# Weight sums of a Strassen quad moved into accumulating DMAs, and the LayerNorm residual moved ahead, in a two-layer decoder trunk on one core

## The chip, the cores and the metric

The kernel runs on one core of one Trainium2 chip. The time is the device time of one execution in microseconds (us): 2227.26 us is the median of three runs of the kernel before, which lie between 2225.66 and 2228.39 us.

## The reference, cut to what matters

Input is x, 256 tokens by 2048. Two layers follow each other; each is a token mixer and then a gated ConvFFN, and after each of the four sub-layers stands `x <- LayerNorm(ALPHA * x + sublayer(x))`. Layer 0 mixes with a gated linear recurrence (HGRN2), layer 1 with a causal spatial gating (gMLP). The change lies in the ConvFFN, which both layers have:

```python
h = x @ w_up                        # 2048 -> 2 * 5632
a, b = split(h, 2)
a = conv_w[0]*a[t-2] + conv_w[1]*a[t-1] + conv_w[2]*a[t] + conv_b
y = (silu(a) * b) @ w_down          # 5632 -> 2048
```

All of it is float32.

## The kernel before, in words

**Number form.** TensorE gets every float32 matrix as two float32r parts, `hi` (the rounded value) and `lo` (what is left), and a product is three matmuls: hi by hi, hi by lo, lo by hi. A weight chunk is 512 by 512 (1 MB). It is loaded into a buffer `raw` by a DMA of SyncE's queue (`begin_fetch`, L96), ScalarE casts it to `whi` in two halves (L120), VectorE subtracts to get `wlo` in two halves (L121). `raw`, `whi` and `wlo` have three buffers each, and `ahead(3)` (L128) issues loads and conversions up to three chunks ahead of the one that TensorE takes. So the conversion of a chunk can begin when TensorE has done with the chunk three places before it.

**The ConvFFN** (`ffn`, L1063) works through eleven F-chunks f of 512 hidden columns, in groups of 4, 3 and 4. For each F-chunk there are two blocks of four weight chunks ("ups"): the gate products for `a` (first `block_b`, L1112) and the products for `b` (second `block_b`, L1116). A block ends in an evacuation by ScalarE and VectorE: `ev_a` (gather, convolution, silu) and `ev_b` (gather, gate, split into `Y`). After a group come the "down" chunks of `w_down`, each 24 matmuls.

**The Strassen quads.** For column chunks 0 and 1 of `w_down` two F-chunks f, f+1 are taken together: the 2x2 blocks B11, B12 (first F-chunk), B21, B22 (second) of the weights against two halves of the tokens, in seven products of 12 matmuls each where eight would be plain (`seven`, L233; `product`, L210). The sums of activations are made by `sums` (L187) into a tile `S`. The sums of weights are made by `make` (L156), in place in two buffers `b11`, `b12` of a pool `qp`, which has one buffer of each. The products are numbered `which`; their order is 0, 1, 2, 3, 4, 6, 5:

- 0: load b11 = B11 and b12 = B12 by SyncE's queue (L154); convert b11; then b11 += b12 on VectorE (two halves, L165)
- 1: convert b11 (B11 + B12)
- 2: load b2 = B22 into a `raw` buffer, convert it; then b11 += b2 and b12 += b2 on VectorE
- 3: convert b11. 4: convert b12 (B12 + B22)
- 6: load b2 = B21; b11 += b2; convert b11. 5: convert b2

**What sets the order.** `ffn_order` (L1023) writes the order of the chunks by hand: ups and downs are counted from 0, and `QUADS` (L34) says behind which count each of the seven products of a quad stands. There are four quads in each layer, so eight in all. The instructions of each engine are laid out once, at build time, mostly in the order of the program, where something whose inputs are planned to be ready may pass something that is not; on the chip each engine runs its list strictly in that order.

**The residual and the memory of `qp`.** `norm` loads the LayerNorm's g and b as eight broadcast tiles into a pool on the right side of the memory. `residual(c)` (L551) applies them to column chunk c of z, four VectorE instructions each (L556, L557), placed behind the last conversion that was issued (`issue_after`). `residual(3)` closes the pool. `qp` opens in the same memory, so the loads of b11 and b12 of a layer's first quad wait for the residual's last instruction. Before, the residual of column chunks 0 and 1 stands behind the second block of F-chunk 0, and that of 2 and 3, with the opening of `qp`, behind the second block of F-chunk 1.

Of the kernel before, what the change touches and what calls it, by code (L numbers as in the profile page):

```python
# [12 lines left out]
ALU = mybir.AluOpType  # L13
# [6 lines left out]
DFF = 5632  # L20
# [5 lines left out]
NB = 512  # L26
CK = 4
# [4 lines left out]
SUMS = ((0, 1), (0, 3), (1, 2), (2, 1))  # L32
SEVEN = (0, 1, 2, 3, 4, 6, 5)
QUADS = (  # L34
# [4 lines left out]
)  # L39
# [12 lines left out]
class Trunk:  # L52
# [96 lines left out]
    def want_seven(self, w, k0, c0, which):  # L149
        self.plan.append((w, k0, c0, None, which))  # L150

    def load_chunk(self, raw, w, k0, c0):
        src = w[k0 * P : (k0 + CK) * P, c0 : c0 + NB].rearrange("(k p) n -> p k n", p=P)
        self.nc.sync.dma_start(raw, src)  # L154

    def make(self):  # L156

        w, k0, c0, _, which = self.plan[self.issued]
        self.issued += 1
        nc = self.nc  # L160

        def add(out, x, y):
            for i in range(0, CK, 2):
                r = slice(i, i + 2)
                nc.vector.tensor_tensor(out[:, r], x[:, r], y[:, r], ALU.add)  # L165

        if which == 0:
            self.b11 = self.qp.tile([P, CK, NB], F32, tag="b11", name="b11")
            self.b12 = self.qp.tile([P, CK, NB], F32, tag="b12", name="b12")
            self.qp.tile([P, PAD2], mybir.dt.uint8, tag="pad2", name="pad2")  # L170
            self.load_chunk(self.b11, w, k0, c0)
            self.load_chunk(self.b12, w, k0, c0 + NB)
        elif which in (2, 6):
            self.b2 = self.wp.tile([P, CK, NB], F32, tag="raw", name="raw")
            self.load_chunk(self.b2, w, k0 + CK, c0 + NB * (which == 2))
        if which == 6:
            add(self.b11, self.b11, self.b2)
        self.convert(
            self.b2 if which in (2, 5) else self.b12 if which == 4 else self.b11, False, False
        )  # L180
        if which == 0:
            add(self.b11, self.b11, self.b12)
        elif which == 2:
            add(self.b11, self.b11, self.b2)
            add(self.b12, self.b12, self.b2)

    def sums(self, act0, act1):  # L187

# [874 lines left out]
    def ffn(self, l, store=None):  # L1063
        nc, tc, a = self.nc, self.tc, self.a
        up, down = a["ffn_w_up"][l], a["ffn_w_down"][l]
        with ExitStack() as st:
            fp = st.enter_context(tc.tile_pool(name=f"fp{l}", bufs=2))
            m = 0
            quads = ExitStack()
            order = self.ffn_order(l)  # L1070
            slots = {}
            self.fresh = {(t, c) for t in range(2) for c in range(4)}

            def sevens():
                while order and order[0][0] == "seven":
                    _, f, which = order.pop(0)
                    self.seven(which, slots[f])

            def next_up(ci):
                assert order.pop(0)[::3] == ("up", ci)  # L1080
                sevens()

            for gi, n in enumerate(FFN_GROUPS):
                acts = []
                for i in range(n):
                    slot = slots[m + i] = FFN_SLOT[gi] + i
                    act = fp.tile([P, 4, S], F32, tag="act", name="act")
                    acts.append(act)

                    def ev_a(j, ps):  # L1090
                        f = 4 * (m + i) + j
                        x = fp.tile([P, S], F32, tag="a", name="a")
                        self.gather(fp, ps, x)
                        cv = act[:, j, :]
                        nc.vector.tensor_scalar(
                            cv, x, self.c(("cw", l, 2), f), self.c(("cb", l), f),
                            ALU.mult, ALU.add,
                        )
                        for d in (1, 2):
                            nc.vector.scalar_tensor_tensor(  # L1100
                                cv[:, d:], x[:, : S - d], self.c(("cw", l, 2 - d), f),
                                cv[:, d:], ALU.mult, ALU.add,
                            )
                        nc.scalar.activation(cv, cv, AF.Silu)

                    def ev_b(j, ps):
                        x = fp.tile([P, S], F32, tag="b", name="b")
                        self.gather(fp, ps, x)
                        nc.vector.tensor_tensor(act[:, j, :], x, act[:, j, :], ALU.mult)
                        self.split(self.Y, 4 * slot + j, act[:, j, :])  # L1110

                    self.block_b(self.X, up, 4, (m + i) * NB, ev_a, halves=m + i == 0,  # L1112
                                 between=next_up)
                    if m + i == 0:
                        self.xps.close()
                    self.block_b(self.X, up, 4, DFF + (m + i) * NB, ev_b, between=next_up)  # L1116
                    if m + i in (0, 1):
                        self.residual(2 * i)
                        self.residual(2 * i + 1)
                    if m + i == 1:  # L1120
                        self.qp = quads.enter_context(
                            tc.tile_pool(name=f"qp{l}", bufs=1, side="right")
                        )
                    if (gi, i) in SUMS:
                        self.sums(*acts[-2:])
                end = m + n == NF // CK
                if end:
                    quads.close()
                    st.close()
                    self.norm("ln2", l, store)  # L1130
                    for c in range(4):
                        fs = [x[1] for x in order if x[2] == c]
                        self.block_a(self.Y, slots[fs[0]] * CK, down, fs[0] * CK, len(fs), c * NB,
                                     self.add_z(c, last=True), staggered=c == 3)
                m += n
                while not end and order[0][0] == "down":
                    _, f, c, first, last = order.pop(0)
                    ch = self.chunk(down, f * CK, c * NB)
                    if first:
                        ps = [self.acc.tile([P, NB], F32, tag="acc", name="pa") for _ in range(2)]  # L1140
                    for t in range(2):
                        self.product(ps[t], self.half(slots[f], t), ch, first, last)
                    if last:
                        for t in range(2):
                            self.gain(t, c, ps[t])
                    sevens()
# [59 lines left out]
```

## Time and profile before

| | |
|---|---|
| median of three runs | 2227.26 us (2225.66 to 2228.39) |
| the profiled execution | 2227.53 us, of which the span from first to last instruction is 2225.8 us |
| TensorE matmul (PE) busy | 2198.7 us, 99% |
| TensorE weight load (PEld) busy | 1896.3 us, 85% |
| VectorE (DVE) busy | 1659.9 us, 75% |
| ScalarE (ACT) busy | 1171.8 us, 53% |
| GpSimd (POOL) busy | 46.8 us, 2% |
| granted TensorE clock, mean | 0.997 |
| DMA | 430.14 MB, 193 GB/s |

Lines of a profile name engine, source line, operation and `out<-in`. In a row of the timeline stand start, length, engine, line, operation, tiles, count, and in brackets the idle time before it with what ended it. In a row of groups stands behind the bar the busy time in us, the mean of one in ns, and the idle time before. In a row of windows stands for each engine busy time with its count, then granted clock (PEclk), DMA share and GB/s. SPq is SyncE's queue, which issues DMAs; L numbers are lines of the kernel.

### The profile page before, as it was taken

The page shows a single profiled execution, that of the slowest core. Times are in us where ns is not written, and L with a number is a line of the kernel's source. Part 1 is how long each engine was busy: PE and PEld are TensorE (multiplying, and loading weights), DVE is VectorE, ACT ScalarE, POOL GpSimd, SP SyncE. Part 2 cuts the span into 40 slices and gives each one's busy share as a digit, 9 for nine tenths or more (in the row PEclk, how much of TensorE's full clock was granted, in tenths as well). Part 3 has the DMA queues.
Part 4 walks back from the last instruction along what each step waited for, and adds up shares of the span by engine and source line. Part 5 has one row for each costly group of instructions (what it writes and reads, how often), then busy time and mean ns, then how long its engine had stood idle before and what let it go on. Part 6 is the DMA issues. An engine that isn't in the chain of part 4 may idle for free.

```text
span 2225.8 us, 31866 instructions
## 1 busy us (share of the span) xinstructions
PE 2198.7 (99%) x12705; PEld 1896.3 (85%) x12705; DVE 1659.9 (75%) x2533; ACT 1171.8 (53%) x1783; POOL 46.8 (2%) x102
## 2 busy tenths in 40 slices
PE   9999999999999999999999999999999999999998
PEld 8888888889788888888888888888788888888886
DVE  6877677668888676877876676567788676877875
ACT  5656575546445454555555545455455454545452
POOL 3000000000000000000000000000000000000000
PEclk9999999999999999999999999999999999999999
DMA  7454645645555665555565665655555656555573
GB/s 269 152 189 143 199 152 170 214 166 188 190 208 189 208 227 190 172 207 189 189 227 187 210 214 192 230 179 172 199 197 190 215 202 207 184 191 174 191 244 114
DMA packets 214597, 430.14 MB, mean 193 GB/s; under 512 B 7577, under 2 KB 9393, under 8 KB 214449
## 3 DMA queue, kind: packets, MB, share of 16 engines
q1 hardware_dynamic: 210080, 415.26, 55.0%
q0 software_dynamic: 4368, 12.85, 1.9%
q8 instruction: 99, 1.62, 0.3%
q14 instruction: 50, 0.40, 0.1%
HBM read 425.98 MB, written 2.10 MB: 192 GB/s over the span
## 4 chain that ended last, share of the span: by engine, by line
PE 92%; DVE 3%; ACT 2%; issue 2%; DMA 1%; POOL 0%; SPq 0%; DVEq 0%; POOLq 0%; ACTq 0%
PE pb L359 36%; PE pb L366 18%; PE pa L215 8%; PE px L215 7%; PE pa L282 6%; PE pa L283 6%; PE pa L281 6%; DVE wlo L121 1%; ACT whi L120 1%; PE pl L796 1%; PE pt L481 1%; DMA b<-in_ffn_w_down_dram 0%; PE pg L1005 0%; DVE z L557 0%; DMA bb<-in_sg_ln_b_dram 0%
## 5 line engine op out<-in xcount | busy, mean ns | idle before, releaser
L359 PE MATMUL pb<-X,whi 128*128 128x512 f32 (+1 forms) x3960 | 1306.1, 384 | 1.9 <-DVE X L495 1.9
L121 DVE TENSOR_TENSOR wlo<-raw,whi 128x1024 fp32r<-128x1024 f32 (+1 forms) x753 | 892.3, 1219 | 450.0 <-ACT whi L120 442.1
L120 ACT CAST whi<-raw 128x1024 fp32r<-128x1024 f32 (+1 forms) x753 | 760.2, 1048 | 697.6 <-PE pb L359 385.9
L366 PE MATMUL pb<-X,wlo 128*128 128x256 f32 x3840 | 1038.0, 278 | 0.0
L359 PEld LDWEIGHTS pb<-X,whi 128*128 128x128 f32 x3960 | 725.7, 188 | 144.0 <-DVE X L495 2.4
L366 PEld LDWEIGHTS pb<-X,wlo 128*128 128x128 f32 x3840 | 713.2, 188 | 7.2 <-DVE wlo L121 0.2
L282 PE MATMUL pa<-wlo,Y 128*128 128x512 f32 x416 | 162.3, 390 | 0.0
L281 PE MATMUL pa<-whi,Y 128*128 128x512 f32 x416 | 162.3, 390 | 0.0
L283 PE MATMUL pa<-whi,Y 128*128 128x512 f32 x416 | 162.0, 389 | 0.0
L215 PE MATMUL pa<-whi,Y 128*128 128x512 f32 x512 | 160.3, 389 | 0.0
L381 ACT COPY rest<-pb 128x256 f32<-128x256 f32 x240 | 87.3, 368 | 97.7 <-PE pb L359 94.7
L215 PEld LDWEIGHTS pa<-whi,Y 128*128 128x128 f32 x512 | 96.1, 188 | 19.7
L121 DVE TENSOR_TENSOR wlo<-b,whi 128x1024 fp32r<-128x1024 f32 x80 | 95.0, 1220 | 14.9 <-ACT whi L120 14.9
L120 ACT CAST whi<-b 128x1024 fp32r<-128x1024 f32 x80 | 80.9, 1050 | 43.0 <-PE pb L359 13.9
L282 PE MATMUL pa<-wlo,X 128*128 128x512 f32 x256 | 99.9, 390 | 0.0
L281 PE MATMUL pa<-whi,X 128*128 128x512 f32 x256 | 99.8, 390 | 0.0
L215 PE MATMUL pa<-wlo,Y 128*128 128x512 f32 x256 | 99.7, 389 | 0.0
L283 PE MATMUL pa<-whi,X 128*128 128x512 f32 x256 | 99.7, 389 | 0.0
L281 PEld LDWEIGHTS pa<-whi,Y 128*128 128x128 f32 x416 | 78.1, 188 | 16.0
L282 PEld LDWEIGHTS pa<-wlo,Y 128*128 128x128 f32 x416 | 78.1, 188 | 16.0
L283 PEld LDWEIGHTS pa<-whi,Y 128*128 128x128 f32 x416 | 78.1, 188 | 15.9
L215 PE MATMUL px<-whi,S 128*128 128x512 f32 x256 | 84.2, 390 | 2.8 <-ACT whi L120 2.8
(191 smaller groups left out, 1816.3 us busy)
## 6 DMA issues: line engine op xcount, KB each, us to landing
raw<-in_ffn_w_up_dram SPq DMA_DIRECT2D x176, 1024.0 KB, 5.0
raw<-in_ffn_w_down_dram SPq DMA_DIRECT2D x72, 1024.0 KB, 4.9
raw<-in_hg_w_in_dram SPq DMA_DIRECT2D x61, 1024.0 KB, 5.0
raw<-in_sg_w_in_dram SPq DMA_DIRECT2D x32, 1024.0 KB, 5.4
raw<-in_hg_w_out_dram SPq DMA_DIRECT2D x16, 1024.0 KB, 4.9
b<-in_ffn_w_down_dram SPq DMA_DIRECT2D x16, 1024.0 KB, 4.9
raw<-in_sg_w_out_dram SPq DMA_DIRECT2D x16, 1024.0 KB, 4.9
g<-in_ln_g_dram POOLq DMA_DIRECT2D x16, 256.0 KB, 5.9
```

Of the source, the lines that this page charges most:

```text
L120: cast = nc.scalar.copy(hi[:, s, :], raw[:, s, :])
L121: self.last_lo = nc.vector.tensor_tensor(lo[:, s, :], raw[:, s, :], hi[:, s, :].bitcast(F32), ALU.subtract)
L215: self.nc.tensor.matmul(ps, x(kk, part), y[:, kk, :], start=start and (kk, part) == (0, 0) and y is hi, stop=stop and (kk, part) == (CK - ...
L281: nc.tensor.matmul(ps[t], xh, hi[:, kk, :], start=n[t] == 0, stop=False)
L282: nc.tensor.matmul(ps[t], xh, lo[:, kk, :], start=False, stop=False)
L283: nc.tensor.matmul(ps[t], xl, hi[:, kk, :], start=False, stop=last)
L359: return self.nc.tensor.matmul(ps[j][:, :, s], ch[0][:, k % CK, c], act[:, k, :, s], start=start and k == 0, stop=k == last, skip_group_ch ...
L366: return self.nc.tensor.matmul(ps[j][:, 1, :], ch[1][:, k % CK, c], act[:, k, 0, :], start=False, stop=False, skip_group_check=loose,)
L381: nc.scalar.copy(r, ps[:, 1, :])
L481: self.last_turn = nc.tensor.transpose(ps[:, j, :], self.z[:, t, k * P : (k + 1) * P], self.ident)
L796: nc.tensor.matmul(ps[n * j : n * j + n, th, :], K[:, own(th, n, j)], moving(th, j), start=True, stop=True, tile_position=(0, n * j),)
```

## The change

Three things are edited. First, two of the four weight sums of a quad become DMAs that add into their destination (`accum_op`), issued by GpSimd: b12 += B22 right behind the load of b12 in step 0, and b11 += B12 behind the conversion of b11 in step 0. The VectorE sums b11 += b12 (step 0) and b12 += b2 (step 2) go; b11 += b2 in steps 2 and 6 stays. Second, `residual(2)`, `residual(3)` and the opening of `qp` move from behind the second block of F-chunk 1 to behind its first block (the gate products). Third, in the first two quads of a layer most of the seven products stand one count later.

```diff
 QUADS = (
-    (0, (17, 19, 22, 24, 26, 28, 30)),
-    (2, (32, 34, 37, 40, 42, 45, 47)),
+    (0, (18, 20, 23, 25, 27, 29, 31)),
+    (2, (33, 35, 38, 40, 43, 45, 47)),
     (5, (65, 67, 70, 73, 76, 79, 82)),
     (7, (89, 91, 94, 96, 98, 100, 102)),
 )
...
-    def load_chunk(self, raw, w, k0, c0):
+    def load_chunk(self, raw, w, k0, c0, add=False):
         src = w[k0 * P : (k0 + CK) * P, c0 : c0 + NB].rearrange("(k p) n -> p k n", p=P)
-        self.nc.sync.dma_start(raw, src)
+        if add:
+            self.nc.gpsimd.dma_start(raw, src, accum_op=ALU.add)
+        else:
+            self.nc.sync.dma_start(raw, src)
...
             self.load_chunk(self.b11, w, k0, c0)
             self.load_chunk(self.b12, w, k0, c0 + NB)
+            self.load_chunk(self.b12, w, k0 + CK, c0 + NB, add=True)
...
         if which == 0:
-            add(self.b11, self.b11, self.b12)
+            self.load_chunk(self.b11, w, k0, c0 + NB, add=True)
         elif which == 2:
             add(self.b11, self.b11, self.b2)
-            add(self.b12, self.b12, self.b2)
...
-                    self.block_b(self.X, up, 4, DFF + (m + i) * NB, ev_b, between=next_up)
-                    if m + i in (0, 1):
-                        self.residual(2 * i)
-                        self.residual(2 * i + 1)
                     if m + i == 1:
+                        self.residual(2)
+                        self.residual(3)
                         self.qp = quads.enter_context(
                             tc.tile_pool(name=f"qp{l}", bufs=1, side="right")
                         )
+                    self.block_b(self.X, up, 4, DFF + (m + i) * NB, ev_b, between=next_up)
+                    if m + i == 0:
+                        self.residual(0)
+                        self.residual(1)
```

## The prediction

> **What bounds the kernel now.** I read the page first, its busy times.
>
> ```profile
> span 2225.8 us, 31866 instructions
> PE 2198.7 (99%) x12705; PEld 1896.3 (85%) x12705; DVE 1659.9 (75%) x2533; ACT 1171.8 (53%) x1783; POOL 46.8 (2%) x102
> ```
>
> TensorE is the bound: all its idle time is 2225.8 - 2198.7 = 27.1 us. The matmuls themselves are not touched by the change, so it can win only what TensorE waits for. The second view is the list of TensorE's own waits; its first line and its fourth carry most of what lies in the ConvFFN.
>
> ```profile
> PE px L215 <- ACT whi L120: 7.1, 4, 2.1
> ...
> PE px L215 <- DVE wlo L121: 1.5, 2, 0.8
> ```
>
> Both are waits of `px`, that is of Strassen products, 8.6 us in six stalls. The third view, the timeline of PE, shows where: in each layer at the first quad only, products 0 and 1. In layer 0:
>
> ```profile
> 602.85 0.39 PE L359 MATMUL pb<-X,whi 128*128 128x512 f32 x1
> 605.37 0.50 PE L215 MATMUL px<-whi,Y 128*128 128x512 f32 x1 [2.13 <-ACT whi L120]
> 606.62 0.50 PE L215 MATMUL px<-wlo,Y 128*128 128x512 f32 x1 [0.76 <-DVE wlo L121]
> ...
> 611.05 0.50 PE L215 MATMUL px<-whi,S 128*128 128x512 f32 x1 [1.62 <-ACT whi L120]
> 611.39 0.28 PE L366 MATMUL pb<-X,wlo 128*128 128x256 f32 x1
> ```
>
> In layer 1:
>
> ```profile
> 1598.36 0.39 PE L359 MATMUL pb<-X,whi 128*128 128x512 f32 x1
> 1600.88 0.50 PE L215 MATMUL px<-whi,Y 128*128 128x512 f32 x1 [2.14 <-ACT whi L120]
> ...
> 1607.83 0.28 PE L366 MATMUL pb<-X,wlo 128*128 128x256 f32 x1
> ```
>
> The price of these two places is the time between the last block matmul and the next one, less what the 13 products between them (12 of product 0, one of product 1) need at full pace. The pace is a row of the chain in an undisturbed stretch:
>
> ```profile
> 712.05 10.88 PE pa L215 x48
> ```
>
> 10.88 / 48 = 0.227 us for one matmul. Layer 0: from 602.85 + 0.227 to 611.39 are 8.31 us, 13 x 0.227 = 2.95 of it work: 5.36 us lost. Layer 1: from 1598.36 + 0.227 to 1607.83 are 9.24 us, less 2.95: 6.29 us lost. Together 11.65 us. That is more than 8.6 since matmuls after a wait also run slower; in layer 1 the windows show why:
>
> ```profile
> 1602.00:1604.00 2.00, 1.86 (x4) 1.49 (x5) 2.00 (x3) 2.00 (x3) 0.00 (x0) 0.50 0.00 0
> ```
>
> The granted clock falls to 0.50 there, and not in layer 0 after the same waits. The Trainium skill ("TensorE: Matmul & The Clock Gate", Part 1) says that the gate judges activity in a free-running window of about 3.4 us, so that it depends on the phase whether such a wait costs clock. By that rule another execution could lose 5.36 or 6.29 at either place, and the sum would be 10.7 to 12.6 us; by the rows it is 11.65, which I take.
>
> **Why TensorE waits there.** The chain is: residual on DVE, load, cast, product. Rows of DVE, the DMA queue and ACT:
>
> ```profile
> 593.29 0.68 DVE L556 TENSOR_TENSOR z<-z,g 128x512 f32<-128x512 f32 x1
> ...
> 598.62 0.69 DVE L557 TENSOR_TENSOR z<-z,b 128x512 f32<-128x512 f32 x1
> 599.45 0.92 SPq L154 DMA_DIRECT2D b<-in_ffn_w_down_dram  x2
> 604.27 2.00 ACT L120 CAST whi<-b 128x1024 fp32r<-128x1024 f32 x2
> ```
>
> The load of b11 is issued 0.14 us after the residual's last addition (598.62 + 0.69 = 599.31), is there at 604.27, and product 0 was due at 603.08. Product 1 then waits for b11's second conversion, bunched up behind.
>
> **The places one count later.** A chunk is 24 matmuls, 24 x 0.227 = 5.44 us. Product 0 of the first quad becomes due at 603.08 + 5.44 = 608.52. Even if the load came as late as now, cast and first `wlo` half would be done near 604.27 + 2.3 = 606.6 (the cast's half to the second product matmul is 606.62 - 604.27 above). So this edit alone takes away the wait of product 0. In the second quad the same shift moves work between chunks that are all ready; no PE wait stands there now, and it costs nothing.
>
> **The residual moved ahead.** Eight DVE instructions that lie at 593 to 599 move to behind `ev_a` of F-chunk 1. What they pass is the conversions of the second block. Rows there, and, as the pattern, the other residual of the layer, which stays:
>
> ```profile
> 554.33 1.29 DVE L557 TENSOR_TENSOR z<-z,b 128x512 f32<-128x512 f32 x2
> 555.54 4.63 DVE L121 TENSOR_TENSOR wlo<-raw,whi 128x1024 fp32r<-128x1024 f32 x4
> ...
> 572.74 1.67 DVE L1100 SCALAR_TENSOR_TENSOR act<-a,cols,act 128x255 f32<-128x255 f32 x4
> 574.32 2.36 DVE L121 TENSOR_TENSOR wlo<-raw,whi 128x1024 fp32r<-128x1024 f32 x2
> ```
>
> There the residual goes first and two chunks' `wlo` wait behind it (x4 at 555.54). At 574.32 I expect the same: eight instructions at 0.60 (the two of 1.29 above overlap a little) are 4.8 us, to 579.1, then the waiting `wlo` with its first half done at 580.3. At that place of the program the conversions up to count 13 are issued, so the waiting one is count 14's. Counts 14 to 17 end at 603.08, where product 0 was due, so TensorE begins count 14 at 603.08 - 4 x 5.44 = 581.3, 1.0 us later than 580.3. I cost it at nothing; if the cover fails it is up to 1 us in each layer, 2 us in all. On SP's queue b11's load then has no one to wait for from 579.1, and the loads of ups queued behind it don't wait with it. The activation sums, which began at 599.35 behind the residual, can begin some 5 us sooner.
>
> **The DVE sums removed.** Of 64 halves of 1.22 us, 32 go: 39 us of DVE. Since no PE wait outside the first quads names DVE's sums, I cost this gain at nothing on the path.
>
> ```profile
> L165 DVE TENSOR_TENSOR b<-b,raw 128x1024 f32<-128x1024 f32 x48 | 56.9, 1220 | 8.3 <-DMA raw<-in_ffn_w_down_dram 8.3
> L165 DVE TENSOR_TENSOR b<-b,b 128x1024 f32<-128x1024 f32 x16 | 19.2, 1218 | 0.0
> ```
>
> **The accumulating DMAs added**, two in each of 8 quads, 1 MB each, on POOL's queue. POOL has nothing else in these stretches, as this window shows (POOL x0), so no one queues behind its two new waits (b12's load; the end of product 0's `wlo`):
>
> ```profile
> 640.00:700.00 60.00, 60.00 (x335) 52.31 (x334) 45.96 (x63) 32.95 (x44) 0.00 (x0) 1.00 0.65 227
> ```
>
> b12's sum is read by product 4 only, seven or more counts later: free. b11's is read by the cast of product 1, and behind that cast on ACT are queued casts of next chunks, evacuation copies and silu. The tightest place is in the third quad; rows of DVE, ACT, PE:
>
> ```profile
> 901.13 1.22 DVE L121 TENSOR_TENSOR wlo<-b,whi 128x1024 fp32r<-128x1024 f32 x1
> 910.87 2.00 ACT L120 CAST whi<-b 128x1024 fp32r<-128x1024 f32 x2 [0.25 <-PE px L215]
> 921.57 0.39 PE L215 MATMUL px<-whi,S 128*128 128x512 f32 x1
> ```
>
> The DMA may start at 901.13 + 1.22 = 902.35. The cast can't come before 910.87 anyway, since it waits for the buffer: 8.5 us are free outright. TensorE needs the first halves at 921.57, 2.3 us behind the cast's start, so the landing may come as late as 919.3, **16.9 us** after its start, before TensorE waits. The trace shows no accumulating DMA. The nearest rows:
>
> ```profile
> b<-in_ffn_w_down_dram SPq DMA_DIRECT2D x16, 1024.0 KB, 4.9
> ...
> wsT<-in_sg_w_s_dram POOLq DMA_DIRECT2D x1, 1024.0 KB, 9.0
> ```
>
> Lower end 4.9 us, the plain load. Upper end 18.0: twice POOL's 1 MB load, if reading and writing the destination doubles the slowest row. I take 9.8 (twice the plain load, close to POOL's 9.0): 1.3 us beyond the free 8.5, a short wait of ACT and none of TensorE. At 18.0 the third and fourth quads (whose steps have the same distances) would cost 1.1 us each, 4.4 us in both layers. The second has more room, by its rows:
>
> ```profile
> 699.73 2.35 DVE L121 TENSOR_TENSOR wlo<-b,whi 128x1024 fp32r<-128x1024 f32 x2
> 722.77 0.39 PE L215 MATMUL px<-whi,S 128*128 128x512 f32 x1
> ```
>
> From 702.08 to 722.77 - 2.3 are 18.4 us. In the first, product 0 is cast when the chunk three places before it ends (608.52 - 2 x 5.44 = 597.6), its `wlo` done some 4 us later behind the activation sums, and product 1 due at 608.52 + 2.72 + 2 x 5.44 = 622.1: 622.1 - 2.3 - 601.7 = 18.1 us. A cost below nothing is excluded: a sum that lands sooner finds the cast waiting for its buffer. The extra traffic is 16 MB plus reading the destinations; the DMA engines are busy by 0.65 in the window above, so the weight loads beside it have a third of the engines' time as room, and I cost that at nothing.
>
> **The sum**, against the profiled execution's own 2227.53 us (span 2225.8 and 1.7 around it): 2227.53 - 5.36 - 6.29 = 2215.9. The median of the runs, 2227.26, lies 0.27 lower: **2215.6 us**. Bounds: another 1 us off where both places had lost clock, 2 us back from the residual, 4.4 us back from the slow end of the DMA. So its own range is 2213.5 to 2222.
>
> **The rivals.**
>
> *Late sums (slower).* The accumulating DMA is handled row by row, lands late, and product 1 of every quad stalls. For it: no row shows such a DMA. Against it: twice any 1 MB row is at most 18.0. The rooms of a layer's four quads add to 18.1 + 18.4 + 2 x 16.9 = 70.3 us. With landing time L the cost of a layer is 4L - 70.3 once all four stall, which eats the gain of 11.65 / 2 = 5.83 at L = 19.0 us. From there it is slower; at L = 22 two layers cost 2 x 17.7 = 35.4 us, less 11.65: 2251 us. Chance 0.15.
>
> *No change.* The stalls go, but L lies between 18.5 and 19.6, or several small ones of 1 us take their place at each of the eight quads (ACT's casts pushed behind the late one): 8 x 1.2 = 9.6 back, 2225 us. For it: ACT must wait at the third and fourth quads already at my 9.8. Against it: by the rows above the cast has 8 us of room (910.87 to 919.3). Chance 0.08.
>
> *Load still late.* The edit doesn't bring b11 sooner, since SP's list keeps it behind other loads. Then the shift by a count still covers it by 608.52 - 606.6 = 1.9 us, and product 1 has a chunk less of room: 2215.6 to 2218, inside the forecast's range. It is no case of its own.
>
> **How the numbers follow.** The measurement of this kernel can tell about 0.2%, 4.5 us, from no change. Forecast 0.77 (2213.5 to 2222, faster), no change 0.08, late sums 0.15. The range goes from 2213 to 2226: it takes in the forecast and most of the no-change case and leaves out the slow one. Faster 0.77, same 0.08, slower 0.15.
>
> **What would show it.** Right: the lines `px L215 <- ACT whi L120` and `<- DVE wlo L121` gone from PE's waits, PE idle near 27.1 - 8.6 = 18.5 us, clock 1.00 through the first quads; L556 and L557 ahead of 581 in layer 0; POOL issues of 1 MB landing in 8 to 12 us; b12 and b11 sums gone from L165 (32 left, all from `raw`); DVE busy near 1621. Wrong: a line `px <- ACT whi` with eight or more times, ACT's `whi<-b` waiting for a DMA by more than 8 us, or a new line `pb <- DVE wlo` near 581, which would say that the residual took its cover away.

## The result and the profile after

The changed kernel takes 2216.35 us, the median of six runs (2213.65 to 2217.13); the kernel before took 2227.14 us in six runs (2225.66 to 2228.39). The ratio is 0.995, with a 95% interval of 0.9937 to 0.9962: faster by 0.5%. 2215.6 us was predicted. The profiled execution took 2217.13 us, its span is 2215.2.

The head of the page after:

```profile
span 2215.2 us, 31922 instructions
PE 2195.3 (99%) x12705; PEld 1894.5 (86%) x12705; DVE 1625.4 (73%) x2501; ACT 1171.1 (53%) x1783; POOL 69.4 (3%) x118
```

TensorE's idle time is now 19.9 us, where it was 27.1, and its busy time has gone down by 3.4 us with the same 12705 matmuls. Of this, 2.3 us lie in layer 1's ConvFFN, where matmuls ran slowly behind the waits; the other 1.1 us lie ahead of layer 0's first convolution, where the change edits nothing. The list of PE's waits after, from its top:

```profile
PE pb L362 <- DVE X L498: 1.9, 2, 1.1
PE pt L484 <- DMA z<-in_x_dram: 1.9, 1, 1.9
PE pb L362 <- DVE a L385: 1.7, 2, 1.3
```

Both lines with `px` are gone. The third line is new: TensorE waits for a bank of PSUM, the memory that holds its products until ScalarE and VectorE evacuate them; VectorE's gather (`a`, L385) has not yet emptied it. The timeline of VectorE after, around the residual, and of the DMA queue:

```profile
573.83 1.30 DVE L559 TENSOR_TENSOR z<-z,g 128x512 f32<-128x512 f32 x2
...
577.44 1.30 DVE L560 TENSOR_TENSOR z<-z,b 128x512 f32<-128x512 f32 x2
578.65 6.90 DVE L121 TENSOR_TENSOR wlo<-raw,whi 128x1024 fp32r<-128x1024 f32 x6
```

```profile
579.21 0.37 SPq L157 DMA_DIRECT2D b<-in_ffn_w_down_dram  x1
```

The residual ends at 578.7 and b11's load is issued at 579.2, 20 us sooner than before; behind the residual the conversions of three chunks run in one piece (x6). Product 0 follows without a wait, at 608.03 (before: 605.37, a count earlier and 2.3 us late):

```profile
608.03 0.39 PE L218 MATMUL px<-whi,Y 128*128 128x512 f32 x1
```

### The profile page after: what moved, and what is told of

It is laid out like the page before. It is cut to its first block, busy times and chain, and to the rows that moved or that the text cites. A ratio compares the mean times of both kernels' runs of the same rounds, so it can differ in the third digit from the quotient of the medians.

```text
span 2215.2 us, 31922 instructions
## 1 busy us (share of the span) xinstructions
PE 2195.3 (99%) x12705; PEld 1894.5 (86%) x12705; DVE 1625.4 (73%) x2501; ACT 1171.1 (53%) x1783; POOL 69.4 (3%) x118
## 4 chain that ended last, share of the span: by engine, by line
PE 92%; DVE 3%; ACT 2%; DMA 2%; issue 1%; POOL 0%; SPq 0%; DVEq 0%; POOLq 0%; ACTq 0%
PE pb L362 36%; PE pb L369 19%; PE pa L218 8%; PE px L218 7%; PE pa L284 6%; PE pa L285 6%; PE pa L286 6%; DVE wlo L121 1%; DMA b<-in_ffn_w_down_dram 1%; ACT whi L120 1%; PE pl L799 1%; PE pt L484 0%; PE pg L1008 0%; DMA bb<-in_sg_ln_b_dram 0%; PE pa L930 0%
## 5 line engine op out<-in xcount | busy, mean ns | idle before, releaser
L120 ACT CAST whi<-b 128x1024 fp32r<-128x1024 f32 x80 | 81.4, 1051 | 66.5 <-DMA b<-in_ffn_w_down_dram 19.9
L218 PEld LDWEIGHTS pa<-whi,Y 128*128 128x128 f32 x512 | 96.1, 188 | 19.9
L286 PEld LDWEIGHTS pa<-whi,Y 128*128 128x128 f32 x416 | 78.1, 188 | 16.1
```

What stands on the lines that cost most here:

```text
L120: cast = nc.scalar.copy(hi[:, s, :], raw[:, s, :])
L218: self.nc.tensor.matmul(ps, x(kk, part), y[:, kk, :], start=start and (kk, part) == (0, 0) and y is hi, stop=stop and (kk, part) == (CK - ...
L286: nc.tensor.matmul(ps[t], xl, hi[:, kk, :], start=False, stop=last)
```

## The experiments

Two numbers are read from each. One is the median against the kernel before, whose median was 2226.45 to 2227.76 us in the different sets. The other is finer: the first 100 us of an execution vary by 2.6 us of TensorE's idle time, and in granted clock from 0.98 to 1.00, between profiles of kernels that are the same there, so each layer's ConvFFN stage is read by itself. Layer 0's goes from the first convolution (`act<-a,cols`) to the first statistics of layer 1's mixer (`vst<-v`); layer 1's interval goes from the mixer's first `y<-pg,bs` to the first store of the output. The two rows of the kernel before that give layer 0's, as an example (first and last start stand behind the durations):

```profile
L1095 DVE TENSOR_SCALAR act<-a,cols x88: 398/407/416, 527.9 to 2124.7; 128x256 f32<-128x256 f32 x88
L961 DVE BATCH_NORM_STATS2 vst<-v x8: 685/690/695, 1242.5 to 1314.1; 128x6 f32<-128x512 f32 x8
```

1242.5 - 527.9 = 714.6 us. For all kernels, each stage from one profiled execution:

| kernel | median us | ratio, 95% interval | layer 0 | layer 1 |
|---|---|---|---|---|
| before | 2227.14 | | 714.6 | 875.0 |
| the change | 2216.35 | 0.995 (0.9937 to 0.9962) | 711.4 | 869.0 |
| places moved only | 2216.95 | 0.9956 (0.9943 to 0.9968) | 710.7 | 870.9 |
| residual moved only | 2214.35 | 0.9941 (0.9927 to 0.9954) | 710.3 | 868.3 |
| DMAs only | 2238.28 | 1.005 (1.0037 to 1.0062) | 721.6 | 881.5 |
| change without DMAs | 2213.47 | 0.9936 (0.9924 to 0.9949) | 709.8 | 868.4 |
| only b12 by DMA | 2214.48 | 0.9941 (0.9929 to 0.9954) | 709.8 | 868.3 |
| only b11 by DMA | 2215.5 | 0.9946 (0.9933 to 0.9958) | 711.9 | 868.5 |
| product 1 later | 2214.89 | 0.9939 (0.9926 to 0.9953) | 709.8 | 868.2 |
| late sums | 2278.25 | 1.0224 (1.0209 to 1.024) | 741.0 | 899.6 |
| plain loads for the DMAs | 2213.83, one execution | | 709.7 | 868.3 |

How well the stages repeat can be read from the four kernels with both moves in which TensorE waits for no late sum (without DMAs, only b12, product 1 later, plain loads): 709.7 to 709.8 and 868.2 to 868.4.

**Each part alone.** Theory A: the gain is the wait for the first quad's load; either of the two moves covers it, and the DMAs bring nothing. Theory B: the parts are needed together, or VectorE's relief carries the gain.

Places only:

```diff
-    (0, (17, 19, 22, 24, 26, 28, 30)),
-    (2, (32, 34, 37, 40, 42, 45, 47)),
+    (0, (18, 20, 23, 25, 27, 29, 31)),
+    (2, (33, 35, 38, 40, 43, 45, 47)),
```

> Only the places of the first two quads move one count later; sums on VectorE, residual where it was. Theory A (the gain is the wait for the first quad's load, and one count of room covers it): product 0 comes due at 608.5 and its load, still issued near 599.5, is converted by 606.6, so both stalls of each layer go and the time is 2215 to 2217 us, ratio about 0.995. Rival B (VectorE is too full there: residual, activation sums and weight sums bunch up): product 0 or 1 still waits, at least 2 us in each layer, and the time is 2220 us or more.

2216.95 us, as theory A has it. The load is issued as late as ever and still comes in time; rows of the DMA queue, ACT and PE:

```profile
600.14 0.92 SPq L154 DMA_DIRECT2D b<-in_ffn_w_down_dram  x2
```

```profile
605.37 2.01 ACT L120 CAST whi<-b 128x1024 fp32r<-128x1024 f32 x2
```

```profile
609.33 0.39 PE L215 MATMUL px<-whi,Y 128*128 128x512 f32 x1
```

The cast begins at 605.37 and product 0 at 609.33 with no wait before it. A wait for `wlo` of 0.46 us is left in each layer. The profiled execution was the slowest of the five, 2221.11 us; in it a wait of 2.4 us in the mixer, which the edit does not touch, ends 0.5 us into layer 1's interval, and from 1332 to 1336 behind it the granted clock is between 0.5 and 0.65.

Residual only:

```diff
-                    self.block_b(self.X, up, 4, DFF + (m + i) * NB, ev_b, between=next_up)
...
                     if m + i == 1:
+                        self.residual(2)
+                        self.residual(3)
                         self.qp = quads.enter_context(...)
+                    self.block_b(self.X, up, 4, DFF + (m + i) * NB, ev_b, between=next_up)
...
```

> Only the residual's second half and the opening of the pool move ahead; places and VectorE sums as before. Theory A: the load is issued near 579 and is there long before product 0 is due at 603.1, so all 11.65 us go too: 2215 to 2216 us. Rival B (the edits are needed together): the activation sums or conversions crowd VectorE behind the second block, product 0 waits 1 us or more, and the time is 2218 us or more.

2214.35 us; all `px` waits are gone. So either move is enough, and the two gains don't add.

The DMAs only:

```diff
+            self.load_chunk(self.b12, w, k0 + CK, c0 + NB, add=True)
...
-            add(self.b11, self.b11, self.b12)
+            self.load_chunk(self.b11, w, k0, c0 + NB, add=True)
...
-            add(self.b12, self.b12, self.b2)
```

> Only the two weight sums go to accumulating DMAs; places and residual as before. Theory A (the DMAs bring no time, and the cast that waits for the sum holds up evacuations queued behind it): the wait of product 0 stays, 3 us in each layer, product 1 no longer is pulled ahead of its turn, and each layer gets a new wait of 1 to 2 us behind the late cast: 2221 to 2230 us, not as fast as the change. Rival B (VectorE's relief of 39 us is what wins): 2217 us or less.

2238.28 us: slower by 0.5%, and by more than theory A had expected. Product 0's wait stays, and in both layers product 1 waits behind it. POOL, ACT and PE in layer 0 of this kernel:

```profile
605.20 2.64 POOL L155 DMA_DIRECT2D b<-in_ffn_w_down_dram  x2 [181.05 <-ACT whi L120]
```

```profile
621.92 1.99 ACT L120 CAST whi<-b 128x1024 fp32r<-128x1024 f32 x2 [14.06 <-DMA b<-in_ffn_w_down_dram]
```

```profile
623.02 0.62 PE L218 MATMUL px<-whi,S 128*128 128x512 f32 x1 [4.88 <-ACT whi L120]
```

Since b11's load comes so late, both accumulating DMAs start together (x2 at 605.20), and the second has landed only 16.7 us later. This is the rival of the late sums, at the first quads: PE's waits for `px` grow from 8.6 to 16.1 us. The two stages are 13.5 us longer than before, 7.6 of them TensorE's idle time; the other 5.9 are longer matmuls, and behind product 1's wait in layer 0 the granted clock is 0.50 from 624 to 630. The moves are what spares the change this, by letting the two start 11 us apart.

The change without its DMAs (both moves, all sums on VectorE):

> The change without its accumulating DMAs: places moved and residual moved, all four weight sums on VectorE. Theory A: the same 11.65 us go and the new wait for a PSUM bank behind the late cast (1.3 us in layer 0, 0.4 in layer 1) is not there, so it is as fast as the change or 1 to 2 us faster: 2214 to 2216 us. Rival B (the removed VectorE sums carry part of the gain): 2219 us or more, with conversions late on VectorE.

2213.47 us, the lowest median here, 2.9 us below the change's. The intervals of the two ratios overlap, so the difference is taken from the stages, 1.6 and 0.6 us. Against the kernel before, the stages have become 4.8 and 6.6 us shorter, 11.4 together: 11.65 was worked out for the two stalls. So the whole gain comes from the moves, and VectorE's 39 us of additions were free.

**What the DMAs cost.** The change gains only 3.2 + 6.0 = 9.2 us in its stages; another 1.1 of its profile lies ahead of them, where the change edits nothing (the first convolution at 526.8, before 527.9): between 5 and 15 us the granted clock was 0.77 and 0.89 in the kernel before, 1.00 in the change. Its rows:

```profile
L1098 DVE TENSOR_SCALAR act<-a,cols x88: 401/408/500, 526.8 to 2114.1; 128x256 f32<-128x256 f32 x88
L964 DVE BATCH_NORM_STATS2 vst<-v x8: 686/690/695, 1238.2 to 1309.7; 128x6 f32<-128x512 f32 x8
```

Its timelines of ACT, DVE and PE in layer 0 show where the rest went:

```profile
608.28 2.00 ACT L120 CAST whi<-raw 128x1024 fp32r<-128x1024 f32 x2 [2.52 <-issue]
614.50 2.00 ACT L120 CAST whi<-b 128x1024 fp32r<-128x1024 f32 x2 [4.23 <-DMA b<-in_ffn_w_down_dram]
616.41 0.63 ACT L384 COPY rest<-pb 128x256 f32<-128x256 f32 x2
```

```profile
615.58 2.36 DVE L121 TENSOR_TENSOR wlo<-b,whi 128x1024 fp32r<-128x1024 f32 x2 [3.26 <-ACT whi L120]
617.86 0.75 DVE L385 TENSOR_TENSOR a<-pb,rest 128x256 f32<-128x256 f32 x2
```

```profile
618.33 0.50 PE L362 MATMUL pb<-X,whi 128*128 128x512 f32 x1 [1.28 <-DVE a L385]
```

The cast of product 1 stands in ACT's list ahead of the four copies that evacuate the block just ended. It waits 4.23 us for the sum; the copies wait behind it, the banks stay full, and TensorE stands still for 1.28 us until 618.33. VectorE's list has the same order: the two halves of `wlo` that need this cast (615.58) stand ahead of the gather, which begins at 617.86 although the first copy is done near 616.8. Product 1 itself begins at 623.25 without a wait. Theory A: the loss is this cast's place. Rival B: traffic, or VectorE's order.

Only b12 by DMA (b11's sum back on VectorE):

```diff
-            self.load_chunk(self.b12, w, k0 + CK, c0 + NB, add=True)
...
-            self.load_chunk(self.b11, w, k0, c0 + NB, add=True)
+            add(self.b11, self.b11, self.b12)
+            self.load_chunk(self.b12, w, k0 + CK, c0 + NB, add=True)
```

> The change with b11 += b12 back on VectorE; only b12 += B22 stays an accumulating DMA, issued behind that addition. Theory A (the change's remaining loss is the cast of product 1 that waits for b11's DMA and holds ACT's queue): no ACT wait for an accumulating DMA, no PE wait for a PSUM bank behind it, time as without any accumulating DMA, 2213 to 2214.5 us. Rival B (the extra traffic of the DMAs slows weight loads or conversions): 2215.5 us or more, with ACT waits for raw loads.

Stages of 709.8 and 868.3, as without DMAs, and no ACT wait for a sum: b12's DMA, which is issued here behind VectorE's sum of b11, is free. The median, 2214.48, is 1 us above that of the kernel without DMAs, which the stages don't show.

Only b11 by DMA:

```diff
-            self.load_chunk(self.b12, w, k0 + CK, c0 + NB, add=True)
...
+            add(self.b12, self.b12, self.b2)
```

> The change with b12 += b2 back on VectorE; only b11 += B12 stays an accumulating DMA. Theory A: the eight ACT waits for the DMA stay (about 2.5 us each) and with them the PE wait for a bank in each layer: 2215 to 2217 us, as the change. Rival B (what costs is the two DMAs together on the 16 engines): as without any, 2213 to 2214 us.

2215.5 us. ACT's waits for the sum are as in the change, and so is the loss, 2.2 us in both layers together; so b12's DMA adds nothing to it. Here nearly all of it lies in layer 0 (711.9), where the one bank wait is:

```profile
ACT whi L120 <- DMA b<-in_ffn_w_down_dram: 19.9, 8, 4.6
```

```profile
PE pb L362 <- DVE a L385: 1.7, 1, 1.7
```

Product 1 of the first quad one count later, with both DMAs:

```diff
-    (0, (18, 20, 23, 25, 27, 29, 31)),
+    (0, (18, 21, 23, 25, 27, 29, 31)),
```

> The change, accumulating DMAs and all, with product 1 of each layer's first quad one count later (21 for 20). By the instruction lists the cast that waits for b11's sum then stands behind the four evacuation copies of its block on ACT, where it stood ahead of them. Theory A (the loss against the kernel without accumulating DMAs is that cast's place): no PE wait for a bank behind VectorE's gather, the ACT wait for the DMA in the first quads gone; layer 0's ConvFFN takes 709.8 us from its first convolution to the first statistics of layer 1's mixer, as without the DMAs, where the change takes 711.4: 2213.5 to 2215 us. Rival B (late sums cost by the DMA traffic or VectorE's order): the bank wait goes, the stage stays at 711 us or more, 2215.5 us or more.

2214.89 us; stages 709.8 and 868.2, and the bank wait is gone. The cast now stands behind the copies:

```profile
616.16 0.37 ACT L384 COPY rest<-pb 128x256 f32<-128x256 f32 x1 [0.99 <-PE pb L362]
616.43 1.06 ACT L120 CAST whi<-b 128x1024 fp32r<-128x1024 f32 x1
```

The DMA traffic is the same as in the change, so the loss of about 2 us was the place of product 1's conversion, as theory A has it, and not the traffic. The run moves the whole conversion: VectorE's two halves of `wlo` stand behind the gathers now, at 620.05. How much of the loss was ACT's order and how much VectorE's it does not tell.

**Late sums.** b11's sum is issued twice, in sequence, so that it lands later; b11 then holds B11 + 2 B12, and the result is not the reference's:

```diff
             self.load_chunk(self.b11, w, k0, c0 + NB, add=True)
+            self.load_chunk(self.b11, w, k0, c0 + NB, add=True)
```

> The change with b11 += B12 issued twice, one behind the other, so that the sum of product 1 lands about 19 us after the first conversion in place of 9.4 (b11 becomes B11 + 2 B12, the products that use it come out otherwise). Theory A (ACT's evacuations queued behind the late cast set the limit, well below 16.9 us): the PE waits grow by most of the added 9.4 us where evacuations stand behind the cast, in the first and fourth quads, and by 1 to 3 us at the others: 2236 to 2256 us. Rival B (only the product's own due time counts, room 16.9 to 18.4 us): 4 x 19 - 70.3 = 5.7 us in each layer, 2226 to 2229 us.

2278.25 us, ratio 1.0224 (1.0209 to 1.024): above both theories. PE's waits:

```profile
PE pb L363 <- DVE a L386: 21.2, 2, 10.9
PE px L219 <- ACT whi L120: 19.0, 6, 4.2
PE px L219 <- DVE wlo L121: 3.7, 6, 0.8
```

Two places are bank waits, in the first quads; the other six are product 1 itself, also in the fourth quads, where theory A expected banks. In the first quad of layer 0 (issues of the two DMAs, then the cast):

```profile
605.13 1.28 POOL L155 DMA_DIRECT2D b<-in_ffn_w_down_dram  x1 [10.06 <-ACT whi L120]
614.78 1.26 POOL L155 DMA_DIRECT2D b<-in_ffn_w_down_dram  x1 [8.38 <-DMA b<-in_ffn_w_down_dram]
```

```profile
624.06 1.99 ACT L120 CAST whi<-b 128x1024 fp32r<-128x1024 f32 x2 [11.43 <-DMA b<-in_ffn_w_down_dram]
```

```profile
628.28 0.80 PE L363 MATMUL pb<-X,whi 128*128 128x512 f32 x1 [10.94 <-DVE a L386]
```

18.9 us from issue to cast cost 10.9 us of TensorE: the first quad's room is 8 us. The change says the same, 9.6 us from 604.88 to the cast at 614.50 and 1.3 of wait. In the third quad the cast waited until 936.57, 21.6 us after `wlo`'s end at 914.99, and product 1 lost 3.36 + 0.76 = 4.1 us: room 17.5, where 16.9 was worked out. The waits add to 43.9 us. The rest of the loss is slower matmuls: TensorE's busy time is 2214.4 us here, 19.1 more than in the change, of which 17.6 lie in the two stages, with a mean granted clock of 0.987 (0.999 there). The ten us around the end of one of the waits, in the fourth quad of layer 0, have a granted clock of 0.66 (the figure ahead of the last two):

```profile
1092.00:1102.00 10.00, 8.47 (x30) 6.64 (x31) 8.95 (x17) 7.84 (x13) 0.00 (x0) 0.66 0.31 101
```

Theory A left out the clock.

**The price of adding.** The sixteen DMAs of the change as plain loads, which overwrite their destination, so that these sums are left out:

```diff
-            self.nc.gpsimd.dma_start(raw, src, accum_op=ALU.add)
+            self.nc.gpsimd.dma_start(raw, src)
```

> The change with the sixteen POOL DMAs as plain loads that overwrite their destination (b12 becomes B22, b11 becomes B12, so the sums are left out). Theory A (reading and adding the destination is about half of the landing time): they land in 5 to 6.5 us, ACT's waits for them vanish, PE's wait for a bank too. Rival B (it is POOL's own issue that is slow, 1.27 us and more): they land in 8 us or more and the waits stay.

One execution of 2213.83 us. ACT waits for none of them and the bank wait is gone, with the cast of product 1 still ahead of the copies: its place costs nothing when the data is there in time. The rows of the change, then of this kernel:

```profile
b<-in_ffn_w_down_dram POOLq DMA_DIRECT2D x16, 1024.0 KB, 9.4
```

```profile
b<-in_ffn_w_down_dram POOLq DMA_DIRECT2D x16, 1024.0 KB, 5.4
```

Adding costs 4.0 us of landing time for 1 MB; a plain load of such a chunk from POOL's queue is 0.5 us slower than SyncE's 4.9.

## Why the prediction was right, and where it failed

- *The total.* 2215.6 us were worked out and 2216.35 measured. This nearness is in part luck: of the 10.6 us between the two spans only 9.2 lie in the stages, where 11.65 had been worked out; the other 1.4 lie where the change edits nothing.
- *The stalls and their price.* Right: 11.65 us were worked out, and without the DMAs' side effect the stages gain 11.4. In layer 1 it was 6.6 for 6.29, in layer 0 4.8 for 5.36.
- *The places one count later take away product 0's wait alone.* Right, shown by the kernel with this edit only: cast at 605.37, product at 609.33. The case "load still late" would have been covered, as said.
- *The residual costs nothing where it goes.* Right: it ended at 578.7 (579.1 expected), and no wait `pb <- DVE wlo` of weight appears (0.4 us of PEld in all).
- *VectorE's 39 us of additions cost nothing on the path.* Right; DVE busy went from 1659.9 to 1625.4 (1621 expected; halves that run back to back overlap a little, six in 6.90 us in the row of 578.65), and the kernels with 64, 48 and 32 halves on VectorE have the same stages where TensorE waits for no late sum.
- *Landing time of an accumulating DMA, 9.8 us.* Measured 9.4 in the median, 8.4 to 11.6. Twice the plain load was a guess that came out near: from the same queue the plain load takes 5.4, so adding makes it 1.7 times as long.
- *"A short wait of ACT and none of TensorE."* This step failed. The room of the first quad was worked out as 18.1 us from product 1's due time alone, and the third quad was taken for the tightest place. The evacuation copies queued behind the cast on ACT were named and not priced, and the DMA starts at 604.88 where 601.7 was worked out. The copies, and the gathers behind `wlo` on VectorE, are due first: the room is 8 us, and with 9.6 us from the issue to the cast TensorE stops in the first quads, which takes 2 us back. In the other quads it is product 1 that TensorE waits for when the sum is late, and in the third the room measured, 17.5 us, is near the 16.9 worked out.
- *The late sums.* They did not come at 9.4 us, but the price was too low: at about 20 us the kernel is 50 us slower than before (2278.25 against 2227.76), where the formula gives 2 x (4 x 20 - 70.3) - 11.65 = 7.8 us. The first quads' room and the clock behind each wait are what it lacked.
- *Another execution could lose clock otherwise* (the rule of the Trainium skill, "TensorE: Matmul & The Clock Gate", Part 1). Of the kernel before there is one profile, so the runs neither show nor exclude it at these two places. They do show that such a wait need not cost clock: of the waits of 2.1 to 2.2 us at product 0 of the first quad, those of layer 0 left the granted clock at 1.00, in the kernel before and in the one with the DMAs only, and those of layer 1 lowered it to 0.50 and 0.57 in windows of 2 us. And the runs of the kernel before have mean granted clocks from 0.994 to 0.998 and times from 2225.1 to 2233.0 us.

What stays open, besides the shares of ACT's and VectorE's order in the loss, is the 1 us between the medians of the kernels with b12's DMA or with the later product 1 (2214.48, 2214.89) and that without DMAs (2213.47). Their stages are equal within 0.2 us, the spreads of their runs are 1.0 to 2.6 us, and their intervals overlap.

## What to carry to other kernels

Before a change of a stage is credited to the engine it relieves, read which wait of the bound engine would go: here 39 us of VectorE were worth nothing, and one load issued some us sooner was worth 11. When an instruction gets a new wait, its room is the smallest due time among all that is queued behind it on its engine, and behind what it feeds on the next engine; here evacuations, on which the next block's banks depend, came due before the data that the instruction itself makes. And an edit of several parts is worth taking apart: the kernel with the lowest median here is the change without the DMAs that its title names first.

## What the runs showed of the hardware

- An accumulating DMA of 1 MB landed in 9.4 us where the plain one from the same queue took 5.4 (medians of sixteen), and its issue held POOL for 1.27 us (0.75 plain). Of two issued back to back the first landed after 8.9 and the second after 16.8 us (layer 1 of the kernel with the DMAs only), nearly one behind the other. Another plain load of 1 MB from POOL's queue, of `wsT`, took 9.0 us; why is not shown.
- The DMA engines' time that the sixteen took was about double. The share of queue q0 was 1.9% without them, and with the same bytes, as adding and as plain DMAs:

```profile
q0 software_dynamic: 12816, 29.63, 6.4%
```

```profile
q0 software_dynamic: 8720, 29.63, 4.0%
```

  4.5% of the engines' span for the sixteen that add, 2.1% for the plain ones; the adding ones also make 8448 packets, the plain ones 4352. The Trainium skill ("DMA: Bandwidth & Descriptors", Rules for kernel authors) says that an accumulating DMA reads its destination and writes it later; the doubled numbers agree with that.
- The granted clock fell to 0.50 for some us at all eight waits of the kernel with late sums, the shortest of them 1.8 us and then 0.8 us. There the two stages are 60.2 us longer than in the change: 42.6 of it is idle time, 17.6 are slower matmuls. So the wait itself was about 70% of the price.
